# Up columns 3 to 20 of a diffusion layer: VectorE's work in one written-out order, the gated rows stored by ScalarE

## The chip, the core and the metric

The kernel runs on one NeuronCore of one Trainium2 chip, as one launch. The metric is the device time of that launch in microseconds (us). Five engines run side by side, each through its own queue in order: TensorE (PE in the profile; its weight loads are PEld), VectorE (DVE), ScalarE (ACT), GpSimd (POOL) and SyncE (SP, which here only issues DMAs). They meet at semaphores.

## What is computed

One layer of a bidirectional hybrid backbone, for 1024 tokens of a noisy latent grid (16 rows of 64) and 128 context tokens (the "prompt"), in float32 with 1024 features. Cut to the part that matters here, the channel mixer:

```
def dw_conv(u, conv_w, conv_b, grid):   # 3x3 over the 16x64 grid, or width 3 over the prompt
    ...
def conv_ffn(h, w_up, conv_w, conv_b, w_down, grid):
    u = dw_conv(h @ w_up, conv_w, conv_b, grid)     # w_up: 1024 x 5632
    gate, up = jnp.split(u, 2, axis=-1)             # 2816 hidden channels each
    return (jax.nn.silu(gate) * up) @ w_down        # w_down: 2816 x 1024
```

Before it come the two scan mixers with their projections, after it the gated residual and a last norm. All of that is the same before and after the change.

## The kernel before

**Stages.** The mixers and projections come first. The up stage (`h @ w_up`, the convolution, the gate) runs from about 768 us of the profiled span to 1260, the down stage (`@ w_down`) from there to the end.

**The up stage** goes over 22 hidden columns of 128 channels (`NHID`; the loop variable is `c`). Channels lie on the 128 partitions, tokens along the free axis. A column has a gate half and an up half, each a product of 1024 features by 128 channels by 1024 tokens. They are computed together, as a 2x2 block product with seven block products in place of eight (Strassen's scheme in Winograd's form), and each block product as three float32r products (high by high, high by low, low by high): 4 feature tiles x 3 = 12 matmuls of 512 tokens. In the trace these are line L1781, and their right-hand sides are named t1, t2, t3, t4, b11, b21, b22. The prompt's products are 24 matmuls of 256 columns a column of channels (L2030), turned by two transposes (L2047).

In the order of TensorE, which is one chain written out (`chained`), a stage of the loop holds: t1 (starts column c's gate half), the two transposes of column c-1's prompt, t4 (ends column c-1's up half), b21, b22, b11 (starts column c's up half), 12 prompt matmuls, t2, 12 prompt matmuls, t3. The last stage, c = 21, puts b11 between the two halves of b22.

**PSUM.** Each half of a column takes one of three buffers `u` in turn. So t1 of column c takes the buffer of column c-2's up half, and b11 of column c that of column c-1's gate half. TensorE's first weight load of t1 therefore waits for VectorE's last tap on column c-2's up half, and that of b11 for its last tap on column c-1's gate half.

**Per column on the other engines.** ScalarE copies three partial sums out of PSUM (`copy`, L1992: p1 after b11, u2 after t2, p5 after t1), makes each half's middle tap with the bias (`conv_middle`, L1946, 1024 tokens; for the prompt in `conv_prompt`, L1977), splits weights into high parts (L1763), and applies Silu to the gate (L2072). VectorE adds the copies back (p1: L2166, u2: L2167, p5: L2196), makes the eight other taps of each half as multiply-adds into an SBUF tile `acc` (`conv_rest`, L1964; taps 0 to 7 run over the kernel's rows and columns without the middle, so taps 3 and 4 have 1008 elements, 1 and 6 have 960, the corners 945), and two prompt taps for each half (L1981, 127 elements). Only after the u2 addition can the gate half's taps begin; the up half's need the p5 addition and t4. GpSimd makes the low parts of the weights (L69) and their sums (L1772 to L1775), multiplies Silu(gate) by up (`second_gate`, L2074), issues the store of the gated rows to DRAM (`scr_g`, L2075), moves one of the down weights' sums (L1911 to L1927) and forms sums over token halves of two columns (L1907 to L1911).

**What sets the order.** The program is recorded in Python's order and a scheduler orders each engine's queue from it; `tc.issue_after(x)` fixes that what follows is issued behind x. TensorE's order is written out; VectorE's, ScalarE's and GpSimd's in columns 3 to 20 are the scheduler's. The convolution's calls for a stage are these:

```
taps = prompt_columns(c - 1)
up(c - 1, 4)
second_half(c - 1)          # second_conv: conv_rows(up half); then second_gate
...
nc.vector.tensor_tensor(S[:, 512:NS], S[:, 0:512], copies["p5"], op=ALU.add)
...
anchor["conv"] = conv_rows(F, c, acc[c][0])
```

`F` is the gate half in PSUM, `S` the up half. `acc` tiles are four, reused two or three columns later.

## Time and profile before

| | us |
|---|---|
| median of 3 runs (lowest, highest) | 1509.09 (1507.84, 1511.35) |
| the profiled execution's own time | 1513.81 |
| its span, first to last instruction | 1512.0 |
| busy in the span: TensorE, VectorE, ScalarE, GpSimd | 1468.2, 1139.9, 782.4, 709.9 |
| 851 to 1234 (383 us, 17 stages of the up loop): TensorE, VectorE, ScalarE, GpSimd busy | 383.0, 371.7, 178.5, 372.7 |
| the same stretch: granted TensorE clock, DMA engines' busy share | 1.00, 0.54 |
| 1234 to 1271 (37 us, the change to the down stage): TensorE, VectorE busy | 34.1, 36.4 |

How to read the rows that follow: a timeline row has start, duration, engine, line, operation, what it writes <- what it reads, shape, and `x` the number of equal instructions that it merges; in brackets the idle time before it and what ended it. A matmul's record runs past the start of the next, since matmuls are pipelined, so distances are taken from start to start. A waits row has the waiting engine and line, what it waited for, the total, the count and the longest.

### The profile page before, as it was taken

What the parts mean: (1) busy time and instruction counts of PE and PEld (TensorE: products, weight loads), DVE (VectorE), ACT (ScalarE), POOL (GpSimd) and SP (SyncE); (2) the same over time, 40 slices, a digit from 0 to 9 for tenths busy, and PEclk for the clock granted to TensorE, in tenths of its full rate; (3) what the DMA queues carried; (4) which work ended last, traced back from release to release, by engine and by line L of the source; (5) the groups of instructions that cost most, each with busy time, mean ns of one, the idle gap of its engine ahead of it and who ended that gap; (6) DMA issues with size and microseconds to landing.
All of it is one profiled execution on the core that took longest, in us unless ns stands there. A gap on an engine that the chain in (4) does not pass through costs nothing.

```text
span 1512.0 us, 31135 instructions
## 1 busy us (share of the span) xinstructions
PE 1468.2 (97%) x12509; PEld 1251.9 (83%) x12509; DVE 1139.9 (75%) x1728; ACT 782.4 (52%) x1524; POOL 709.9 (47%) x541
## 2 busy tenths in 40 slices
PE   6999999999999999999999999999999999999998
PEld 2799998999898988777788888888888877888886
DVE  3766565674565767755799999999999999689475
ACT  3665567555454555513775444444444444466444
POOL 1612122334333241222339999999999996000001
PEclk9999999999999999999999999999999999999999
DMA  9311121335535363967652655554654667979762
GB/s 338 137 44 48 39 61 54 113 102 186 147 105 176 116 195 129 335 230 253 205 175 91 193 148 146 139 138 121 197 124 130 173 175 203 381 254 370 236 192 115
DMA packets 173802, 253.79 MB, mean 168 GB/s; under 512 B 11828, under 2 KB 113698, under 8 KB 171738
## 3 DMA queue, kind: packets, MB, share of 16 engines
q1 hardware_dynamic: 150455, 173.52, 36.0%
q0 software_dynamic: 22592, 77.60, 16.7%
q8 instruction: 98, 1.61, 0.4%
q10 hardware_dynamic: 611, 0.68, 0.1%
q14 instruction: 46, 0.38, 0.1%
HBM read 191.93 MB, written 82.90 MB: 182 GB/s over the span
## 4 chain that ended last, share of the span: by engine, by line
PE 81%; DMA 5%; DVE 4%; ACT 3%; POOL 3%; issue 2%; SPq 0%; POOLq 0%; ACTq 0%; DVEq 0%
PE u L1781 24%; PE mm L625 15%; PE xb L2317 7%; PE mm L639 6%; PE yb L2317 6%; PE x L2030 4%; PE mm L777 3%; PE lv L964 3%; PE yb L2371 2%; PE u L1545 2%; PE x L1032 2%; PE mm L519 1%; DMA raw<-in_w_in_dram 1%; PE ada L1201 1%; DMA wa<-in_w_ada_dram 1%
## 5 line engine op out<-in xcount | busy, mean ns | idle before, releaser
L1964 DVE SCALAR_TENSOR_TENSOR acc<-u,convc,acc 128x945 f32<-128x945 f32 (+2 forms) x352 | 426.6, 1218 | 7.4 <-ACT acc L1946 0.5
L69 POOL TENSOR_TENSOR wl<-raw,wh 128x1024 fp32r<-128x1024 f32 x42 | 102.9, 2462 | 248.3 <-ACT wh L133 193.1
L625 PE MATMUL mm<-h1h,wh 128*128 128x384 f32 x528 | 185.1, 350 | 0.9 <-ACT qj L528 0.9
L625 PE MATMUL mm<-h1l,wh 128*128 128x384 f32 x528 | 179.0, 339 | 0.0
L625 PE MATMUL mm<-h1h,wl 128*128 128x384 f32 x528 | 179.0, 339 | 0.0
L927 DVE TENSOR_TENSOR Q<-Q,fb 128x384 f32<-128x384 f32 x126 | 83.9, 666 | 84.6 <-PE lv L964 83.9
L69 POOL TENSOR_TENSOR wul<-ra,wuh 128x1024 fp32r<-128x1024 f32 (+1 forms) x45 | 113.2, 2516 | 22.2 <-ACT wuh L1763 15.7
L69 POOL TENSOR_TENSOR wul<-sr,wuh 128x512 fp32r<-128x512 f32 (+1 forms) x64 | 115.9, 1812 | 6.6 <-ACT wuh L1763 6.5
L917 ACT ACTIVATE m<-k 128x384 f32<-128x384 f32 x126 | 70.2, 557 | 82.4 <-PE lv L964 38.6
L2281 POOL TENSOR_TENSOR sq<-sq,mhalf 128x1 f32<-128x1 f32 x9 | 11.0, 1230 | 207.4 <-DVE sq L2280 207.4
L625 PEld LDWEIGHTS mm<-h1h,wh 128*128 128x128 f32 x528 | 99.4, 188 | 5.7 <-issue 3.9
L625 PEld LDWEIGHTS mm<-h1l,wh 128*128 128x128 f32 x528 | 99.5, 189 | 0.6 <-issue 0.2
L625 PEld LDWEIGHTS mm<-h1h,wl 128*128 128x128 f32 x528 | 99.3, 188 | 0.8 <-issue 0.5
L639 PE MATMUL mm<-wh,h1h 128*128 128x256 f32 x288 | 84.4, 293 | 0.0
L929 DVE TENSOR_TENSOR k<-k,fb 128x384 f32<-128x384 f32 x126 | 74.1, 588 | 10.8 <-ACT m L917 6.0
L639 PE MATMUL mm<-wh,h1l 128*128 128x256 f32 x288 | 81.2, 282 | 0.0
L639 PE MATMUL mm<-wl,h1h 128*128 128x256 f32 x288 | 81.0, 281 | 0.0
L133 ACT ACTIVATE wh<-raw 128x1024 fp32r<-128x1024 f32 x50 | 52.8, 1058 | 37.4 <-PE mm L625 11.8
L1992 ACT ACTIVATE u2p<-u 128x512 f32<-128x512 f32 x44 | 26.4, 599 | 71.1 <-PE u L1781 70.1
L2074 POOL TENSOR_TENSOR acc<-acc,acc 128x1152 f32<-128x1152 f32 x22 | 60.3, 2742 | 6.1 <-DVE acc L1964 4.9
L1763 ACT ACTIVATE wuh<-ra 128x1024 fp32r<-128x1024 f32 (+1 forms) x43 | 44.4, 1034 | 34.7 <-issue 15.7
L1763 ACT ACTIVATE wuh<-sr 128x512 fp32r<-128x512 f32 (+1 forms) x63 | 48.7, 773 | 22.6 <-PE x L2030 17.1
(385 smaller groups left out, 4471.6 us busy)
## 6 DMA issues: line engine op xcount, KB each, us to landing
ra<-in_w_ffn_up_dram SPq DMA_DIRECT2D x84, 256.0 KB, 3.1
raw<-in_w_in_dram SPq DMA_DIRECT2D x32, 512.0 KB, 4.6
v<-in_w_ada_dram SPq DMA_DIRECT2D x27, 512.0 KB, 4.9
scr_g<-acc POOLq DMA_DIRECT2D x22, 576.0 KB, 6.2
scr_s<-late POOLq DMA_DIRECT2D x11, 1024.0 KB, 8.1
scr_t<-in_w_ffn_down_dram POOLq DMA_DIRECT2D x16, 704.0 KB, 7.4
wa<-in_w_ada_dram SPq DMA_DIRECT2D x16, 512.0 KB, 5.9
scr_t<-in_w_ffn_down_dram POOLq DMA_DIRECT2D x2, 2816.0 KB, 12.6
```

What stands on the lines that cost most here:

```text
L69: return eng.tensor_tensor(out, full, hi.bitcast(F32), op=ALU.subtract)
L625: anchor["fill"] = mm(ps, a[:, kt, :], h[kt][b], start=(n == 0), stop=(n == 23))
L639: anchor["fill"] = mm(ps, h[kt][t // 3][:, ts_], a[:, kt % 4, :], start=(n == 0), stop=(n == 23))
L917: nc.scalar.activation(aps(t, 0, [[2 * h, NB], [h, 2], [1, h]]), aps(src, 0, [[2 * h, NB], [BL + h, 2], [1, h]]), AF.Copy)
L927: nc.vector.tensor_tensor(qm, qm, aps(ff_, 2 * h - 1, [[BL - h, 2], [2 * h, NB], [0, h]]), op=ALU.mult)
L929: nc.vector.tensor_tensor(km, km, aps(ff_, BL + 2 * h - 1, [[-(BL + h), 2], [2 * h, NB], [0, h]]), op=ALU.mult)
L1763: return lambda: nc.scalar.activation(hi, raw, AF.Copy), lambda eng: split_lo(eng, lo, raw, hi)
L1781: last = mm(dst, w_slot(c, a, x)[:, kt, :], HB[y][b][:, kt, :], start=(start and n == 0), stop=(stop and n == 11), skip_group_check=True,)
L1964: last = nc.vector.scalar_tensor_tensor(o, u3[:, r0 + dy : r1 + dy, c0 + dx : c1 + dx], wc(3 * (dy + 1) + dx + 1), o, op0=ALU.mult, op1=AL ...
L2030: last = mm(pk, HB[h]["p"][:, 4 * half + kt, :], aps(flat(W[x]), a * 512 + kt * P, [[(b - a) * 512, 2], [1, P]]), start=(half + kt + n == ...
L2074: last = anchor["gate"] = nc.gpsimd.tensor_tensor(accg, accg, accu, op=ALU.mult)
L2317: anchor["down"] = mm(banks[i][:, cs], w[a][:, ts_], w[b][:, 512 + cs.start : 512 + cs.stop], start=(start and j == 0 and n == 0), stop=(j ...
```

## The change

It concerns columns 3 to 20 (`FIXED`). Their VectorE instructions are issued in one chain (`vec`): each one is recorded behind the one before. `conv_prompt` is cut into its middle and its two taps, so that they can be placed apart. The gate half's prompt taps stay on either side of the gate's tap 3; the up half's two prompt taps move from the gate's last taps to behind the up half's taps 0 and 1; and the up half's tap 3 moves ahead of the p1 addition. ScalarE makes the gate half's middle tap ahead of the split of the weights s2 and s4 (before, behind it). The store of column c-1's gated rows goes from GpSimd's queue, where it stands some instructions behind the product, to ScalarE's queue, where it stands ahead of column c's Silu; columns 20, 21 and 0 to 2 keep the store on GpSimd. No instruction of TensorE or SyncE moves, and no operation is added or taken away.

VectorE's queue, from the gate half's tap 4 of column 15 (tile acc_10300) to the next column's p1 addition (`u<-u,cp`); acc_10299 is column 15's up half. Before:

```order
L1964 SCALAR_TENSOR_TENSOR acc_10300<-u,convc,acc_10300 128x16x63
L1964 SCALAR_TENSOR_TENSOR acc_10300<-u,convc,acc_10300 128x15x63
L1981 SCALAR_TENSOR_TENSOR acc_10299<-x,convc,acc_10299 128x127
L1964 SCALAR_TENSOR_TENSOR acc_10300<-u,convc,acc_10300 128x960
L1981 SCALAR_TENSOR_TENSOR acc_10299<-x,convc,acc_10299 128x127
L1964 SCALAR_TENSOR_TENSOR acc_10300<-u,convc,acc_10300 128x15x63
L1964 SCALAR_TENSOR_TENSOR acc_10299<-u,convc,acc_10299 128x15x63
L1964 SCALAR_TENSOR_TENSOR acc_10299<-u,convc,acc_10299 128x960
L1964 SCALAR_TENSOR_TENSOR acc_10299<-u,convc,acc_10299 128x15x63
L2166 TENSOR_TENSOR u<-u,cp_10253 128x512
```

The same piece of the changed kernel:

```order
L1964 SCALAR_TENSOR_TENSOR acc_10300<-u,convc,acc_10300 128x16x63
L1964 SCALAR_TENSOR_TENSOR acc_10300<-u,convc,acc_10300 128x15x63
L1964 SCALAR_TENSOR_TENSOR acc_10300<-u,convc,acc_10300 128x960
L1964 SCALAR_TENSOR_TENSOR acc_10300<-u,convc,acc_10300 128x15x63
L1964 SCALAR_TENSOR_TENSOR acc_10299<-u,convc,acc_10299 128x15x63
L1984 SCALAR_TENSOR_TENSOR acc_10299<-x,convc,acc_10299 128x127
L1964 SCALAR_TENSOR_TENSOR acc_10299<-u,convc,acc_10299 128x960
L1984 SCALAR_TENSOR_TENSOR acc_10299<-x,convc,acc_10299 128x127
L1964 SCALAR_TENSOR_TENSOR acc_10299<-u,convc,acc_10299 128x15x63
L1964 SCALAR_TENSOR_TENSOR acc_10299<-u,convc,acc_10299 128x16x63
L2075 TENSOR_TENSOR u<-u,cp_10253 128x512
```

The gate's last tap comes two instructions sooner, and one tap more (the up half's tap 3) stands before the p1 addition. From the p1 addition to the gate's tap 4 the order is the old one, without that tap. The changed order is the same in each of the 17 stages.

ScalarE's queue in the changed kernel, from the gate half's middle tap of column 15 to the next p1 copy:

```order
L1946 ACTIVATE acc_10300<-u,vcol,convc 128x1024
L1763 ACTIVATE wuh<-sr 128x2x512
L1763 ACTIVATE wuh<-sr 128x512
L2000 ACTIVATE u2p_10305<-u 128x512
L1976 ACTIVATE acc_10300<-x,vcol,convc 128x128
L1763 ACTIVATE wuh<-ra 128x2x512
L1946 ACTIVATE acc_10299<-u,vcol,convc 128x1024
L1976 ACTIVATE acc_10299<-x,vcol,convc 128x128
L2091 DMA scr_g_133<-acc_9783 128x1152
L2092 ACTIVATE acc_10300<-acc_10300 128x1152
L2000 ACTIVATE cp_10253<-u 128x512
```

Before, the first two rows stand the other way round and the DMA row is missing; acc_9783 holds column 14's gated rows.

The diff:

```diff
--- before.py
+++ after.py
@@ -1971,16 +1971,24 @@
             )
         return last
 
+    def prompt_middle(pp, ch, acc):
+        bc = vcol[:, col["conv_b"] + ch : col["conv_b"] + ch + 1]
+        return nc.scalar.activation(
+            acc[:, NS:NT], pp, AF.Identity, bias=bc, scale=convc[:, 4 * 44 + ch : 4 * 44 + ch + 1]
+        )
+
+    def prompt_tap(pp, ch, acc, dx):
+        c0, c1 = max(0, -dx), min(P, P - dx)
+        o = acc[:, NS + c0 : NS + c1]
+        t = (4 + dx) * 44 + ch
+        return nc.vector.scalar_tensor_tensor(
+            o, pp[:, c0 + dx : c1 + dx], convc[:, t : t + 1], o, op0=ALU.mult, op1=ALU.add
+        )
+
     def conv_prompt(pp, ch, acc):
-        wc = lambda t: convc[:, t * 44 + ch : t * 44 + ch + 1]
-        bc = vcol[:, col["conv_b"] + ch : col["conv_b"] + ch + 1]
-        nc.scalar.activation(acc[:, NS:NT], pp, AF.Identity, bias=bc, scale=wc(4))
+        prompt_middle(pp, ch, acc)
         for dx in (-1, 1):
-            c0, c1 = max(0, -dx), min(P, P - dx)
-            o = acc[:, NS + c0 : NS + c1]
-            nc.vector.scalar_tensor_tensor(
-                o, pp[:, c0 + dx : c1 + dx], wc(3 + dx + 1), o, op0=ALU.mult, op1=ALU.add
-            )
+            prompt_tap(pp, ch, acc, dx)
 
     u, pks = {}, {}
 
@@ -2039,6 +2047,58 @@
 
         chained(products)
 
+    FIXED = range(3, NHID - 1)
+
+    def vec(fn):
+        with tc.issue_after(anchor["vec"].ins) if "vec" in anchor else nullcontext():
+            anchor["vec"] = fn()
+
+    def gate_tap(c, i):
+        vec(lambda: conv_rest(u[c][0], c, acc[c][0], part=slice(i, i + 1)))
+
+    def up_tap(c, i):
+        vec(lambda: conv_rest(u[c][1], 22 + c, acc[c][1], part=slice(i, i + 1)))
+
+    def turn_prompt(c):
+        pp = ps_p.tile([P, 2, P], F32, name="x", tag="x")
+
+        def turned():
+            for i in range(2):
+                last = nc.tensor.transpose(pp[:, i, :], pt_t[:, i * P : (i + 1) * P], ident)
+            return last
+
+        chained(turned)
+        up_first = SLOT[c]["21"] < SLOT[c]["11"]
+        return (pp[:, 1 if up_first else 0, :], c, acc[c][0]), (pp[:, 0 if up_first else 1, :], 22 + c, acc[c][1])
+
+    def add_to(dst, a, nm):
+        return nc.vector.tensor_tensor(dst, a, copies[nm], op=ALU.add)
+
+    def fixed_rest(c):
+
+        gate_p, up_p = turn_prompt(c)
+        up(c, 4)
+        prompt_middle(*gate_p)
+        prompt_tapped(gate_p, -1)
+        gate_tap(c, 3)
+        prompt_tapped(gate_p, 1)
+        for i in range(4, 8):
+            gate_tap(c, i)
+        conv_middle(u[c][1], 22 + c, acc[c][1])
+        last = prompt_middle(*up_p)
+        if c - 1 in FIXED:
+            with tc.issue_after(last.ins):
+                nc.scalar.dma_start(scr_g[c - 1], gs[c - 1])
+        nc.scalar.activation(acc[c][0], acc[c][0], AF.Silu)
+        for i, dx in enumerate((-1, 1)):
+            up_tap(c, i)
+            prompt_tapped(up_p, dx)
+        up_tap(c, 2)
+        up_tap(c, 3)
+
+    def prompt_tapped(pp, dx):
+        vec(lambda: prompt_tap(*pp, dx))
+
     def prompt_columns(c):
         pp = ps_p.tile([P, 2, P], F32, name="x", tag="x")
 
@@ -2068,11 +2128,13 @@
     def second_gate(c):
 
         accg, accu = acc[c]
-        with after("p1") if c == 0 else nullcontext():
-            nc.scalar.activation(accg, accg, AF.Silu)
+        if c not in FIXED:
+            with after("p1") if c == 0 else nullcontext():
+                nc.scalar.activation(accg, accg, AF.Silu)
         gs[c] = accg
         last = anchor["gate"] = nc.gpsimd.tensor_tensor(accg, accg, accu, op=ALU.mult)
-        nc.gpsimd.dma_start(scr_g[c], accg)
+        if c + 1 not in FIXED or c not in FIXED:
+            nc.gpsimd.dma_start(scr_g[c], accg)
         if sums_todo and c > 0:
             with tc.issue_after(last.ins):
                 sums_todo.pop(0)()
@@ -2116,6 +2178,8 @@
             up(c - 1, 4)
             prompt_columns(c - 1)
             second_half(c - 1)
+        elif c - 1 in FIXED:
+            fixed_rest(c - 1)
         elif c > 0:
             taps = prompt_columns(c - 1)
             up(c - 1, 4)
@@ -2161,6 +2225,14 @@
             up(c, 7)
             up_prompt(c, 0)
             first_sums()
+        elif c - 1 in FIXED:
+            vec(lambda: add_to(F[:, 0:512], F[:, 0:512], "p1"))
+            up_tap(c - 1, 4)
+            up_tap(c - 1, 5)
+            vec(lambda: add_to(F[:, 512:NS], F[:, 512:NS], "u2"))
+            up_tap(c - 1, 6)
+            up_tap(c - 1, 7)
+            second_gate(c - 1)
         else:
             with after("second") if c < 3 else nullcontext():
                 nc.vector.tensor_tensor(F[:, 0:512], F[:, 0:512], copies["p1"], op=ALU.add)
@@ -2183,8 +2255,10 @@
             run("act", copy_pt)
         else:
             copy_pt()
+        if c in FIXED:
+            anchor["mid"] = conv_middle(F, c, acc[c][0])
         if c > 0 and n:
-            with tc.issue_after(anchor["copy"].ins) if c == 1 else nullcontext():
+            with after("mid") if c in FIXED else tc.issue_after(anchor["copy"].ins) if c == 1 else nullcontext():
                 split_slots(n, ("s2", "s4"), nc.gpsimd)
         if c == 1:
             with tc.issue_after(anchor["copy"].ins):
@@ -2193,8 +2267,14 @@
         if c > 0:
             if not last_c:
                 up(c, 7)
-            nc.vector.tensor_tensor(S[:, 512:NS], S[:, 0:512], copies["p5"], op=ALU.add)
-        if c > 0:
+            if c in FIXED:
+                gate_tap(c, 0)
+                vec(lambda: add_to(S[:, 512:NS], S[:, 0:512], "p5"))
+                gate_tap(c, 1)
+                gate_tap(c, 2)
+            else:
+                nc.vector.tensor_tensor(S[:, 512:NS], S[:, 0:512], copies["p5"], op=ALU.add)
+        if c > 0 and c not in FIXED:
             with after("second") if c < 3 else nullcontext():
                 anchor["conv"] = conv_rows(F, c, acc[c][0])
         if c > 0 and n:
```

## The prediction

> **What bounds the kernel now.** I read the page, then the table by stages, the list of waits in the up stage, and last the timelines of one stage on each engine. First the page's head, the row by stages for 851 to 1234 (time, then busy us and count of TensorE, weight loads, VectorE, ScalarE, GpSimd, granted clock, DMA share, GB/s), and two rows of the waits between 828 and 1300:
>
> ```profile
> span 1512.0 us, 31135 instructions
> 851.00:1234.00 383.00, 383.00 (x1875) 317.02 (x1874) 371.70 (x393) 178.48 (x240) 372.68 (x249) 1.00 0.54 149
> PEld u L1781 <- DVE acc L1964: 7.9, 18, 1.7
> PEld u L1781 <- PE u L1781: 4.6, 18, 0.3
> ```
>
> By busy time TensorE has nothing to give: 383.0 of 383. But its records overlap, and a weight load that waits shows only as a gap between loads. There are 18 such waits on a VectorE tap, one a stage, and 18 more that the profile puts down to TensorE itself. So I go by distances from start to start (TensorE; the last row is stage 21):
>
> ```profile
> 817.18 0.39 PE L1781 MATMUL u<-b11h,wuh 128*128 128x512 f32 x1
> 819.90 0.28 PE L2030 MATMUL x<-wuh,ph 128*128 128x256 f32 x1
> ...
> 851.33 0.47 PE L1781 MATMUL u<-t1h,wuh 128*128 128x512 f32 x1
> ...
> 1110.08 0.50 PE L1781 MATMUL u<-b11h,wuh 128*128 128x512 f32 x1
> 1112.95 0.28 PE L2030 MATMUL x<-wuh,ph 128*128 128x256 f32 x1
> 1121.29 0.47 PE L1781 MATMUL u<-t1h,wuh 128*128 128x512 f32 x1
> 1124.10 0.27 PE L2047 MATMUL x<-ident,late 128*128 128x128 f32 x1
> 1132.52 0.50 PE L1781 MATMUL u<-b11h,wuh 128*128 128x512 f32 x1
> 1233.68 0.47 PE L1781 MATMUL u<-t1h,wuh 128*128 128x512 f32 x1
> 1245.01 0.50 PE L1781 MATMUL u<-b11h,wuh 128*128 128x512 f32 x1 [1.28 <-DVE acc L1964]
> ```
>
> From the t1 of stage 4 to that of stage 21 there are 17 stages in 1233.68 - 851.33 = 382.35 us, 22.49 each. In stage 2, where b11 found its buffer free, its twelve matmuls took 819.90 - 817.18 = 2.72. In the stage shown the same twelve took 2.87 (1110.08 to 1112.95), and t1's twelve 2.81 (1121.29 to 1124.10). From b11 to b11 that stage took 22.44. Without those two stalls (0.15 and 0.09) it would take 22.20; the matmul ahead of each is stretched by some hundredths too, so 22.16 to 22.20 is TensorE's own pace (an estimate from these rows).
>
> Who is late is seen on VectorE, over the same stretch:
>
> ```profile
> 1113.78 0.70 DVE L2166 TENSOR_TENSOR u<-u,cp 128x512 f32<-128x512 f32 x1 [0.15 <-ACT cp L1992]
> ...
> 1118.10 0.69 DVE L2167 TENSOR_TENSOR u<-u,u2p 128x512 f32<-128x512 f32 x1
> 1118.70 3.69 DVE L1964 SCALAR_TENSOR_TENSOR acc<-u,convc,acc 128x960 f32<-128x960 f32 x3
> 1122.30 0.69 DVE L2196 TENSOR_TENSOR u<-u,u2p 128x512 f32<-128x512 f32 x1
> 1122.90 2.45 DVE L1964 SCALAR_TENSOR_TENSOR acc<-u,convc,acc 128x960 f32<-128x960 f32 x2
> 1125.28 0.35 DVE L1981 SCALAR_TENSOR_TENSOR acc<-x,convc,acc 128x127 f32<-128x127 f32 x1
> ...
> 1126.98 2.49 DVE L1964 SCALAR_TENSOR_TENSOR acc<-u,convc,acc 128x1008 f32<-128x1008 f32 x2
> 1129.62 0.35 DVE L1981 SCALAR_TENSOR_TENSOR acc<-x,convc,acc 128x127 f32<-128x127 f32 x1 [0.15 <-ACT acc L1977]
> 1129.89 1.21 DVE L1964 SCALAR_TENSOR_TENSOR acc<-u,convc,acc 128x960 f32<-128x960 f32 x1
> 1131.02 0.34 DVE L1981 SCALAR_TENSOR_TENSOR acc<-x,convc,acc 128x127 f32<-128x127 f32 x1
> 1131.27 4.79 DVE L1964 SCALAR_TENSOR_TENSOR acc<-u,convc,acc 128x945 f32<-128x945 f32 x4
> 1136.21 0.70 DVE L2166 TENSOR_TENSOR u<-u,cp 128x512 f32<-128x512 f32 x1
> ```
>
> The gate's last tap is the first of the four at 1131.27; at 1.19 it ends at 1132.46, and b11 begins at 1132.52. That closes a loop: p1 addition at 1113.78, gate's last tap done 18.68 later, b11 0.06 after that, its 2.87, the copy by ScalarE, next p1 addition at 1136.21. Round it takes 22.43, and **this loop, not a full engine, sets the stage**. VectorE itself waits twice in it, at 1129.62 and before 1136.21 (the four taps end at 1136.06). A tap that is followed by an unrelated instruction hands over 0.08 before its record ends (1129.89 + 1.21 against 1131.02), so each 0.15 of idle is 0.23 lost, and VectorE's own work is about 22.43 - 0.46 = 21.97. It fits under TensorE's 22.2.
>
> **The change part by part.** I call a the time at which the p1 addition could start if only TensorE and ScalarE decided; in the stage shown it is 1113.78. ScalarE's rows there:
>
> ```profile
> 1117.31 0.60 ACT L1992 ACTIVATE u2p<-u 128x512 f32<-128x512 f32 x1 [1.17 <-PE u L1781]
> ...
> 1119.00 1.06 ACT L1763 ACTIVATE wuh<-sr 128x1024 fp32r<-128x1024 f32 x1
> 1119.95 1.20 ACT L1946 ACTIVATE acc<-u,vcol,convc 128x1024 f32<-128x1024 f32 x1
> ...
> 1124.79 0.45 ACT L1977 ACTIVATE acc<-x,vcol,convc 128x128 f32<-128x128 f32 x1
> ...
> 1129.15 0.45 ACT L1977 ACTIVATE acc<-x,vcol,convc 128x128 f32<-128x128 f32 x1
> 1132.56 1.17 ACT L2072 ACTIVATE acc<-acc 128x1152 f32<-128x1152 f32 x1 [2.97 <-DVE acc L1964]
> ```
>
> 1. *VectorE's order up to b11.* Two times are fixed by TensorE through ScalarE: the u2 addition not before 1117.31 + 0.60 + 0.03 = 1117.94, a + 4.16; the gate's first prompt tap not before 1124.79 + 0.45 + 0.04 = 1125.28, a + 11.50, or a + 11.41 once t1 has lost its 0.09. From the u2 addition the order is the old one: 4.20 to the p5 addition (1118.10 to 1122.30), 2.98 to the first prompt tap (to 1125.28); that is a + 11.34, so it waits until 11.41. Then 1.70 to behind the second prompt tap (1125.28 to 1126.98) and now four gate taps in a row: 2.49 for two, and 2.45 - 1.21 = 1.24 for each of two more, 4.97. The gate is done at a + 18.09 instead of 18.68. The two prompt taps and their wait are gone from in front of it: 0.6 sooner. With a stage of 22.20, b11's load is due at a + 22.20 - 0.83 (b11's end to a, 1112.95 to 1113.78) - 2.72 - 0.23 (a load runs one matmul ahead, 2.72/12) = a + 18.42. The tap's end plus the 0.06 gives 18.15. **Spare 0.27: the wait of b11 goes.**
>
> 2. *VectorE's order round to the next p1 addition.* From the gate's last end: -0.08, tap 1.12 (3.60 for the three of 1118.70, less two at 1.24), prompt 0.26, tap 1.13 (1129.89 to 1131.02), prompt 0.26, two taps 2.41 (2.49 less 0.08): 5.10. So the p1 addition comes at a + 23.19, 0.99 behind the next a. Then 0.61 and two taps, 2.41: the u2 addition could start 4.01 after that a, and is held until 4.16. VectorE keeps up, with 0.15 to spare.
>
> 3. *t1.* Its buffer is freed by the up half's tap 7, the second of the three at 1118.70, which ends at 1121.15, a + 7.37. Now that is a + 4.16 + 0.60 + 1.24 + 1.20 = 7.20. 0.17 sooner against a stall of 0.09: it goes too, though with little to spare.
>
> 4. *ScalarE's middle tap sooner.* It moves ahead of a weight split of 1.06: it can start at 1119.00 instead of 1119.95 and is done at 1120.20, a + 6.42, and the split ends 1.1 later. The gate's tap 0, which needs the middle, comes at a + 4.16 + 0.60 + 2 x 1.24 = 7.24: no wait. GpSimd gets the high parts 1.1 later; see 5.
>
> 5. *The store.* GpSimd's rows, and a store issued by ScalarE elsewhere in the program:
>
> ```profile
> 1124.37 2.71 POOL L2074 TENSOR_TENSOR acc<-acc,acc 128x1152 f32<-128x1152 f32 x1
> 1132.59 1.04 POOL L2075 DMA_DIRECT2D scr_g<-acc  x1
> 40.07 0.36 ACTq L578 DMA_DIRECT2D scr_lr<-lrs  x1
> ```
>
> On ScalarE one issue costs between 0.36 and GpSimd's 1.04; I take 0.4, the row of the same engine. It stands between 1129.60 and the Silu at 1132.56, which waits 2.97 for VectorE (2.4 in the new order): hidden. It waits for the product, done at 1127.08, 2.5 before it; behind it on ScalarE are the Silu and the p1 copy, a further 3.5 away (the copy is due 0.63 before the next a, at 1135.35; less 1129.6, 1.17 and 1.04). Without this cover of 6.0 every us of lateness would move a. GpSimd loses 1.04 of issue and its split work starts at most 1.1 later: as much as nothing. I take 0 for 4 and 5, with +0.2 a stage as the bad end if GpSimd falls behind, and no gain as the good end, since TensorE waits for neither.
>
> 6. *Stage 21.* Here b11 comes half a product sooner and waits 1.28 us (row 1245.01). The gate of column 20 is done 0.6 sooner: 0.6 gained.
>
> Sum: 17 x (22.49 - 22.20) = 4.9, plus 0.6: **5.5 us**. It has to pass the change to the down stage, where the chain of waits runs
>
> ```profile
> 1245.01 4.39 PE u L1781 x18
> ...
> 1251.87 2.85 DMA raw<-in_w_ffn_down_dram
> ```
>
> that is, from TensorE's own up products to the first down weights, so what starts it is what comes sooner. The profiled execution took 1513.8 (span 1512.0 and 1.8 around it), 4.7 above the median of the runs; less 5.5 it would be 1508.3, and the median 1509.1 becomes **1503.6 us**.
>
> **Rivals.**
> - *The wait only moves.* VectorE has 0.15 of spare at the u2 addition. If an instruction in 1. or 2. costs some tenths more (a wait for two semaphores, a prompt tap late), t1's load waits for tap 7 instead: a stage of 22.35 gives 17 x 0.14 + 0.6 = 3.0, 1506.1. For it: the 0.15. Against: the new order has the same number of taps that directly follow one of their own tile, eight a stage. Up to no gain, 1509.1.
> - *GpSimd becomes the pace (slower).* It is busy 372.7 of 383, 21.9 a stage. If the split that comes 1.1 later idles it each stage and the missing issue doesn't pay that back, its round grows to 22.7; after some columns the product is more than 6.0 late, the store holds ScalarE's p1 copy, and all follow: 17 x 0.2 = +3.4, 1512.5. The point is a round over 22.49. Against: 21.9 - 1.0 + 1.1 is 22.0.
> - *The gain is lost at the down stage*, if the down weights or their sums (moved by GpSimd's queue) come at their own pace: 1508.5. Against: the chain above has TensorE before the DMA.
> - *TensorE's pace is not 22.2.* If 2.72 for twelve matmuls were itself some stall that eases, VectorE's 21.97 would be the limit: 17 x 0.52 + 0.6 = 9.4, 1499.7. Against: the twelve of row 817.18 waited for nothing and took 2.72. The Trainium skill's page "TensorE: Matmul & The Clock Gate", section "Wait — 56ns, not 53.3ns?", puts a warm matmul of 512 columns at 215.7 ns; here it is 2.72/12 = 227 ns at a granted clock of 1.00, so the trace disagrees and decides; by the page's figure a stage would be shorter than VectorE's 21.97, which is this rival's time.
>
> **How the numbers follow.** Forecast 0.73; the wait only moves 0.14; GpSimd 0.05; lost at the down stage 0.05; TensorE faster 0.03. Range 1501.6 to 1508.2: below, TensorE at 22.16 (6.2 gained) and 1.3 for the scatter of a median of three (the runs shown lie 3.5 apart); above, the first rival to most of its way. About 0.2%, 3.0 us, is what a measurement tells from no change. Faster: the forecast but 0.02, the last rival, 0.03 of the first: 0.77. Slower: GpSimd and 0.01 of the first: 0.06. Same: 0.17.
>
> **What would show it.** Right: stages of 22.2 from t1 to t1; no wait of b11's load on VectorE from stage 4 to 20, b11's twelve matmuls at 2.72; VectorE's p1 addition about 1 us behind its copy, and a short wait for ScalarE at the u2 addition and the prompt tap; stage 21's wait near 0.7; ScalarE's wait before Silu shorter, with a DMA issue in it. Wrong: stages at 22.4 or more with t1's load waiting (first rival), GpSimd without idle time and ScalarE waiting for its product (second), or stages of 22.2 with the first down product no sooner (third).

## The result, and the profile after

| | before | after |
|---|---|---|
| median of 19 runs each, on one chip (lowest, highest), us | 1511.76 (1507.84, 1514.93) | 1505.80 (1501.69, 1508.60) |
| ratio after to before, 95% interval | | 0.9962 (0.9954 to 0.9970) |
| the profiled execution: span, us | 1512.0 | 1504.1 |
| t1 of stage 4 to t1 of stage 21, us | 382.35 | 378.40 |

The change is worth 0.38% (0.30 to 0.46), 5.7 us of 1510; 5.5 were forecast. The forecast median of 1503.6 is missed by 2.2: it was counted down from the median of the three runs that were shown, 1509.09, which lies 2.7 below that of the nineteen. What was forecast well is the difference between the kernels. The row by stages of the changed kernel for 849 to 1227 (columns as before):

```profile
849.00:1227.00 378.00, 377.11 (x1870) 318.45 (x1869) 369.15 (x392) 177.85 (x239) 361.61 (x232) 1.00 0.55 150
```

And its waits of TensorE's weight loads between 828 and 1300:

```profile
PEld u L1781 <- DVE u L2276: 2.5, 1, 2.5
PEld u L1781 <- DVE acc L1964: 2.2, 2, 1.1
PEld u L1781 <- POOL wul L69: 1.3, 1, 1.3
PEld u L1781 <- PE u L1781: 0.3, 1, 0.3
```

The 18 waits on a VectorE tap (7.9 us) have become two, in stages 3 and 21, outside the stretch of stages 4 to 20; the 18 that the profile put down to TensorE itself (4.6 us) have become one. Two are new, once each, 2.5 and 1.3 us: they come below. TensorE from start to start (rows picked out, as in the prediction):

```profile
849.21 0.47 PE L1781 MATMUL u<-t1h,wuh 128*128 128x512 f32 x1
...
1105.65 0.39 PE L1781 MATMUL u<-b11h,wuh 128*128 128x512 f32 x1
1108.38 0.28 PE L2038 MATMUL x<-wuh,ph 128*128 128x256 f32 x1
1116.69 0.40 PE L1781 MATMUL u<-t1h,wuh 128*128 128x512 f32 x1
1119.44 0.38 PE L2067 MATMUL x<-ident,late 128*128 128x128 f32 x2
1127.85 0.39 PE L1781 MATMUL u<-b11h,wuh 128*128 128x512 f32 x1
1227.61 0.40 PE L1781 MATMUL u<-t1h,wuh 128*128 128x512 f32 x1
```

b11 to b11 takes 22.20 in the stage shown, b11's twelve 2.73 (2.87 before), t1's twelve 2.75 (2.81 before). Seventeen stages take 378.40, 22.26 each; without stage 7, which took 23.36, the mean is 22.19. The reason is on GpSimd and TensorE:

```profile
914.76 1.31 POOL L1909 TENSOR_TENSOR late<-acc 128x512 f32<-128x512 f32 x1 [3.54 <-DMA scr_s<-late]
917.35 0.50 PE L1781 MATMUL u<-t1h,wul 128*128 128x512 f32 x1 [0.89 <-POOL wul L69]
```

GpSimd stood 3.54 us because a store of the token sums had not yet left their tile, and the low half of t1's weights, next in its queue, came late. A second execution of the same kernel (below) has no such stage, so it does not belong to the order: 1.2 us by chance in one execution.

VectorE over the stage shown, from its p1 addition to the next, and ScalarE beside it:

```profile
1110.20 0.69 DVE L2075 TENSOR_TENSOR u<-u,cp 128x512 f32<-128x512 f32 x1
1110.80 2.50 DVE L1964 SCALAR_TENSOR_TENSOR acc<-u,convc,acc 128x1008 f32<-128x1008 f32 x2
1113.37 0.70 DVE L2075 TENSOR_TENSOR u<-u,u2p 128x512 f32<-128x512 f32 x1
...
1118.04 2.44 DVE L1964 SCALAR_TENSOR_TENSOR acc<-u,convc,acc 128x960 f32<-128x960 f32 x2
1120.62 0.35 DVE L1984 SCALAR_TENSOR_TENSOR acc<-x,convc,acc 128x127 f32<-128x127 f32 x1
...
1122.32 6.09 DVE L1964 SCALAR_TENSOR_TENSOR acc<-u,convc,acc 128x1008 f32<-128x1008 f32 x5
1128.33 0.34 DVE L1984 SCALAR_TENSOR_TENSOR acc<-x,convc,acc 128x127 f32<-128x127 f32 x1
...
1132.38 0.69 DVE L2075 TENSOR_TENSOR u<-u,cp 128x512 f32<-128x512 f32 x1
```

```profile
1108.57 0.60 ACT L2000 ACTIVATE cp<-u 128x512 f32<-128x512 f32 x1 [2.19 <-PE u L1781]
...
1112.73 0.60 ACT L2000 ACTIVATE u2p<-u 128x512 f32<-128x512 f32 x1 [1.16 <-PE u L1781]
...
1120.13 0.45 ACT L1976 ACTIVATE acc<-x,vcol,convc 128x128 f32<-128x128 f32 x1
...
1122.62 0.33 ACTq L2091 DMA_DIRECT2D scr_g<-acc  x1
...
1127.39 1.17 ACT L2092 ACTIVATE acc<-acc 128x1152 f32<-128x1152 f32 x1 [2.46 <-DVE acc L1964]
```

The p1 copy ends at 1109.17, so a is 1109.21, and the p1 addition now comes 0.99 us behind a. Against the times worked out from a: u2 addition a + 4.16 (forecast 4.16), gate's first prompt tap a + 11.41 (11.41), next p1 addition a + 23.17 (23.19). The gate's last tap is the fourth of the five at 1122.32; the fifth, of 1.19, ends at 1128.41 and starts 0.08 before the fourth's record ends, so the gate is done at 1127.30, a + 18.09 (18.09). b11's load starts 0.31 us later without having waited. VectorE's own two waits can be read here too: the two taps before the u2 addition end at 1113.30, and it starts at 1113.37, 0.04 behind the end of ScalarE's copy; the two gate taps at 1118.04 end at 1120.48, and the prompt tap starts at 1120.62, 0.04 behind the end of ScalarE's middle tap. They are 0.07 and 0.14.

**The end of the up columns changed too, which nothing in the prediction speaks of.** GpSimd (POOL), VectorE and TensorE about column 21's end, first after, then before:

```profile
1238.28 0.50 PE L1781 MATMUL u<-b11h,wuh 128*128 128x512 f32 x1 [0.72 <-DVE acc L1964]
...
1247.99 2.39 POOL L69 TENSOR_TENSOR wul<-ra,wuh 128x1024 fp32r<-128x1024 f32 x1 [5.91 <-ACT wuh L133]
1248.03 3.43 DVE L69 TENSOR_TENSOR wl<-ra,wh 128x1024 fp32r<-128x1024 f32 x1
1253.23 0.50 PE L1781 MATMUL u<-t4h,wuh 128*128 128x512 f32 x1 [2.29 <-DVE u L2276]
```

```profile
1254.50 1.21 DVE L69 TENSOR_TENSOR wl<-ra,wh 128x1024 fp32r<-128x1024 f32 x1
1254.71 3.28 POOL L69 TENSOR_TENSOR wul<-ra,wuh 128x1024 fp32r<-128x1024 f32 x1 [6.51 <-DMA raw<-in_w_ffn_down_dram]
1268.40 2.77 POOL L69 TENSOR_TENSOR wul<-sr,wuh 128x1024 fp32r<-128x1024 f32 x1
1271.23 0.50 PE L2317 MATMUL xb<-wul,wuh 128*128 128x512 f32 x1 [1.77 <-POOL wul L69]
```

Here VectorE and GpSimd both make low halves of down weights, each a subtraction of two SBUF tiles. Before, VectorE's started 0.21 us ahead of GpSimd's: VectorE's took 1.21, GpSimd's 3.28 instead of 2.4. After, GpSimd's started 0.04 us ahead: it took 2.39 and VectorE's 3.43. Whoever is second takes longer by nearly as much as the first still has to run. The Trainium skill's page "SBUF — State Buffer", section "Who interferes with whom", says that a VectorE instruction with two SBUF inputs contends with a GpSimd instruction that reads SBUF, because its second input comes through a shared read interface, and that the order of issue decides who is blocked. These rows agree. VectorE's delay holds back column 21's p5 addition, and with it TensorE's t4 by 2.29 us. In exchange TensorE no longer waits for GpSimd's low half of the fourth down pair, where it had lost 1.77 us by its own row, 2.16 from matmul to matmul: having come 2.3 us later, it finds it ready. One stall took the other's place.

The two spans differ by 8.0, more than the change is worth. Stage 0 starts at 768.05 before and at 765.97 after: 2.1 us of work that nothing here touches. Some 1.6 lie in the down stage, where the execution before had a lower granted clock for a moment (the figure before the last two; its row for 1256 to 1300):

```profile
1256.00:1300.00 44.00, 42.19 (x185) 34.31 (x184) 38.80 (x32) 18.23 (x22) 27.35 (x15) 0.96 0.84 250
```

The same row of after:

```profile
1256.00:1300.00 44.00, 43.96 (x196) 36.04 (x194) 38.10 (x31) 19.43 (x22) 20.72 (x13) 1.00 0.90 279
```

From the first down matmul on, the execution before took 251.55, where a kernel below with the same wait and a clock of 1.00 (store_only) took 249.96. The 4.3 that are left and the 1.2 of stage 7 make 5.5. From here on stages are compared with stages and runs with runs, not spans.

### The profile page after: what moved, and what is told of

Same layout as the page of the kernel before. It is cut to its first block, busy times and chain, and to the rows that moved or that the text cites. A ratio compares the mean times of both kernels' runs of the same rounds, so it can differ in the third digit from the quotient of the medians.

```text
span 1504.1 us, 31108 instructions
## 1 busy us (share of the span) xinstructions
PE 1460.4 (97%) x12509; PEld 1251.7 (83%) x12509; DVE 1139.8 (76%) x1728; ACT 783.2 (52%) x1524; POOL 699.7 (47%) x524
## 4 chain that ended last, share of the span: by engine, by line
PE 80%; DVE 5%; DMA 5%; ACT 3%; issue 3%; POOL 2%; SPq 0%; POOLq 0%; ACTq 0%; DVEq 0%
PE u L1781 23%; PE mm L625 15%; PE xb L2397 8%; PE yb L2397 6%; PE mm L639 5%; PE x L2038 3%; PE mm L777 3%; PE lv L964 3%; PE yb L2451 2%; PE u L1545 2%; DVE acc L1964 2%; PE x L1032 2%; PE mm L519 2%; DMA wa<-in_w_ada_dram 1%; PE ada L1201 1%
```

## Experiments

The theory: b11's wait on VectorE's last gate tap, and with it t1's wait on the up half's last tap, is all that the change removed; the store and the middle tap are neutral. "Stage" is the mean over the 17 stages from stage 4's t1 to stage 21's, from each kernel's profile; the medians of one block come from one chip and share the runs of the kernel before.

| kernel | median, us (runs) | kernel before beside it (runs) | ratio, 95% | t1 of stages 4 and 21 | stage |
|---|---|---|---|---|---|
| prompt_back | 1509.26 (11) | 1510.21 (28) | 0.9994 (0.9984 to 1.0003) | 849.04, 1230.03 | 22.41 |
| tap3_back | 1506.70 (11) | | 0.9980 (0.9971 to 0.9990) | 847.67, 1227.20 | 22.33 |
| store_back | 1507.68 (6) | | 0.9972 (0.9960 to 0.9983) | 851.36, 1228.58 | 22.19 |
| store_only | 1510.02 (11) | | 0.9994 (0.9985 to 1.0003) | 847.05, 1229.17 | 22.48 |
| late_middle | 1505.67 (11) | 1510.75 (23) | 0.9971 (0.9962 to 0.9980) | 851.21, 1228.46 | 22.19 |
| extra_one | 1504.88 (6) | | 0.9972 (0.9960 to 0.9983) | 847.85, 1225.10 | 22.19 |
| end_after | 1504.37 (6) | | 0.9966 (0.9954 to 0.9978) | 848.53, 1225.84 | 22.20 |
| end_before | 1508.77 (11) | | 0.9988 (0.9977 to 0.9999) | 848.50, 1230.73 | 22.48 |
| after_again | 1505.19 (6) | 1510.57 (16) | 0.9970 (0.9959 to 0.9982) | 851.70, 1228.97 | 22.19 |
| wide | 1504.22 (5) | | 0.9955 (0.9942 to 0.9967) | 849.53, 1227.39 | 22.23 |
| extra_three | 1508.80 (10) | | 0.9990 (0.9979 to 1.0001) | 848.18, 1228.29 | 22.36 |

### The up half's prompt taps back among the gate's taps

```diff
-        for i in range(4, 8):
+        for i in range(4, 6):
             gate_tap(c, i)
         ...
+        for i in (6, 7):
+            prompt_tapped(up_p, 2 * i - 13)
+            gate_tap(c, i)
         nc.scalar.activation(acc[c][0], acc[c][0], AF.Silu)
-        for i, dx in enumerate((-1, 1)):
-            up_tap(c, i)
-            prompt_tapped(up_p, dx)
-        up_tap(c, 2)
+        for i in range(3):
+            up_tap(c, i)
```

> The changed kernel with one part undone: the two prompt taps of the up column go back among the gate's last taps (between taps 5, 6 and 7, as before the change); the rest of the order, the store on ScalarE and the early middle tap stay. Theory (b11 waited for VectorE's last gate tap, and moving these two taps behind it is what freed it): they put the gate's end back by 2 x 0.26 = 0.52 us, with 0.1 to 0.2 more if the prompt tap waits for ScalarE's middle tap again; b11's load has 0.30 us to spare in the changed kernel, so it waits 0.2 to 0.45 us in every stage from 4 to 20. Stages go from 22.19 back to 22.4 to 22.6, b11's twelve from 2.72 to 2.85, and the time from 1505.8 to 1509.5 to 1512, that is most of the gain is lost. Rival one (the gain comes from moving the store from GpSimd to ScalarE): 1505 to 1507, stages stay at 22.2. Rival two (the gain comes from the up column's fourth tap ahead of the first addition): the same, 1505 to 1507.

The gain is gone: 0.9994, an interval that holds 1; the median, 1509.26, lies just under the expected 1509.5. The stages are at 22.41, and the waits of TensorE's loads between 828 and 1300 say which half of the loss this is:

```profile
PEld u L1781 <- DVE acc L1964: 8.4, 19, 1.7
PEld u L1781 <- PE u L1781: 0.3, 1, 0.3
```

b11's wait on the gate's last tap is back in every stage, t1's is not. So the two prompt taps' place is worth 22.41 - 22.19 = 0.22 us a stage, and both rivals fall: the store and the early tap 3 are still in this kernel and save only 22.49 - 22.41 = 0.08.

### The up half's tap 3 back behind the p1 addition

```diff
         up_tap(c, 2)
-        up_tap(c, 3)
 ...
             vec(lambda: add_to(F[:, 0:512], F[:, 0:512], "p1"))
+            up_tap(c - 1, 3)
             up_tap(c - 1, 4)
```

> The changed kernel with the other part of VectorE's order undone: the up column's tap 3 goes back behind the p1 addition, so that the addition comes one tap (1.18 us) sooner in VectorE's order. Theory: the addition then starts as soon as ScalarE's copy is there, about 0.05 to 0.1 us after it rather than 1.0, VectorE stands still for 0.1 to 0.2 us there, and the u2 addition comes 0.2 us later than the 1.18 us it would gain; the gate's end moves by +0.1 to +0.3 us against its copy. b11's 0.30 us of spare is used up or nearly: stages of 22.2 to 22.35 and 1505.5 to 1508.5. Rival (only the prompt taps' place counts, tap 3 is neutral): 1505 to 1506.5 and stages of 22.19. Rival (tap 3 ahead of the addition is the whole gain): stages of 22.45 and 1510.

Time and stage lie inside what was expected, but the mechanism is another one. The waits of VectorE (849 to 1227) and of TensorE's loads (828 to 1300):

```profile
DVE u L2075 <- ACT cp L2000: 4.3, 17, 0.3
PEld u L1781 <- PE u L1781: 4.6, 18, 0.3
```

VectorE's two additions in one stage:

```profile
1108.10 0.70 DVE L2075 TENSOR_TENSOR u<-u,cp 128x512 f32<-128x512 f32 x1 [0.25 <-ACT cp L2000]
1112.43 0.69 DVE L2075 TENSOR_TENSOR u<-u,u2p 128x512 f32<-128x512 f32 x1
```

b11 does not wait at all. The p1 addition now waits for its copy (0.25 us, in all 17 stages), and with three taps between, the u2 addition comes 4.33 after it, 0.17 behind the a + 4.16 of the changed kernel. The up half's last taps follow the u2 addition, and t1 waits for them again, with the same 18 waits and 4.6 us as in the kernel before. So tap 3 ahead of the addition is what frees t1. Of the 0.14 a stage (22.33 - 22.19), 0.11 lies there: from start to start, in the mean of the stages, t3's twelve take 2.77 where the changed kernel has 2.75, and t1's 2.83 where it has 2.75, both as in the kernel before. The other 0.03 lies in t4's twelve (2.85 where the kernel before and the changed one have 2.83), for which no wait is listed; its cause stays open. The two parts, 0.22 and 0.11, make 0.33 where both together saved 0.30.

### The store: back on GpSimd, and alone on ScalarE

```diff
-        if c - 1 in FIXED:
-            with tc.issue_after(last.ins):
-                nc.scalar.dma_start(scr_g[c - 1], gs[c - 1])
 ...
-        if c + 1 not in FIXED or c not in FIXED:
-            nc.gpsimd.dma_start(scr_g[c], accg)
+        nc.gpsimd.dma_start(scr_g[c], accg)
```

> The changed kernel with the gated rows' stores put back on GpSimd's queue for all columns; VectorE's order and the early middle tap stay. Theory (the store's place is neutral): stages of 22.19 and 1505 to 1507; ScalarE's start of the up column's middle tap moves by up to 0.3 us with no one waiting for it. Rival (the store on ScalarE carries a part of the gain, because GpSimd has 0.6 us more per stage for the weights' low halves): 1508 to 1510, with TensorE waits for GpSimd's low halves in several stages.

In the other kernel the order is that of before, and the store alone goes to ScalarE:

```diff
-            conv_prompt(pp[:, 0 if up_first else 1, :], 22 + c, acc[c][1])
+            last = conv_prompt(pp[:, 0 if up_first else 1, :], 22 + c, acc[c][1])
+            if c - 1 in FIXED and c in FIXED:
+                with tc.issue_after(last.ins):
+                    nc.scalar.dma_start(scr_g[c - 1], gs[c - 1])
 ...
-        nc.gpsimd.dma_start(scr_g[c], accg)
+        if c + 1 not in FIXED or c not in FIXED:
+            nc.gpsimd.dma_start(scr_g[c], accg)
```

> The kernel before with only the stores moved from GpSimd to ScalarE (behind the up column's prompt middle tap), VectorE's order left to the planner as before. Theory (neutral): 1510.5 to 1513 with stages of 22.45 to 22.55 and b11's load waiting in every stage as before. Rival (the store is the gain): 1506 to 1508 with stages below 22.35.

The stages are 22.19 and 22.48: those of the changed kernel and of the kernel before. With the store alone the waits of TensorE's loads are the old ones:

```profile
PEld u L1781 <- DVE acc L1964: 8.0, 19, 1.7
PEld u L1781 <- PE u L1781: 4.6, 18, 0.3
```

The store's place is neutral in the stages. The medians miss a little: store_back lies 0.7 us over the expected 1507, with an interval that holds the changed kernel's ratio, and store_only, 1510.02, 0.5 under the expected 1510.5, with an interval that holds 1.

### ScalarE's middle tap back behind the split

```diff
-        if c in FIXED:
-            anchor["mid"] = conv_middle(F, c, acc[c][0])
         if c > 0 and n:
-            with after("mid") if c in FIXED else ...:
+            with ...:
                 split_slots(n, ("s2", "s4"), nc.gpsimd)
         ...
+            if c in FIXED:
+                conv_middle(F, c, acc[c][0])
```

> The changed kernel with ScalarE's middle tap of the gate's image rows put back behind the high half of slots s2 and s4 (1.05 us). Theory: VectorE's order needs the middle tap sooner, since gate tap 0 now starts 0.65 us after the middle tap's end; put back, gate tap 0 waits 0.3 to 0.5 us in every stage, of which VectorE's own slack (0.07 at the u2 addition, 0.13 at the prompt tap) and b11's spare 0.30 take most: stages 22.2 to 22.4 and 1506 to 1509. Rival, the step as forecast (the middle tap's place is worth nothing): stages of 22.19 and 1505 to 1506.5.

The stages stay at 22.19, so the theory here was wrong and the rival, the step as forecast, held. VectorE's waits between 849 and 1227 show why it was close:

```profile
DVE acc L1964 <- ACT acc L1946: 3.7, 16, 0.3
```

Gate tap 0 does wait now, some 0.2 us in 16 stages, and that is covered by the time in which VectorE would otherwise have waited at the prompt tap and by b11's spare.

### One and three more instructions ahead of the gate's end

```diff
         for i in range(4, 8):
+            if i == 7:
+                o = gate_p[0][:, 0:127]
+                vec(lambda: nc.vector.scalar_tensor_tensor(
+                    o, o, convc[:, c : c + 1], acc[c][0][:, NS : NS + 127], op0=ALU.mult, op1=ALU.add))
             gate_tap(c, i)
```

In the second kernel the condition is `i > 4`.

> The changed kernel with one more prompt-sized VectorE instruction (128 x 127, 0.26 us) ahead of the gate's last tap in columns 3 to 20; it writes a tile that nobody reads any more, so the results are the same. Theory: VectorE's work in a stage is 21.98 of 22.19 us; with 0.26 more it is 22.24 and becomes the pace, while b11's spare of 0.30 is just not used up: stages of 22.24 to 22.33, 1506.8 to 1508.3, and the wait is t1's load on the up column's last tap, not b11's. Rival (VectorE has more room than its two waits show): stages of 22.19, 1505 to 1506.5. Rival (b11's spare is smaller than its 0.30 us): b11's load waits in every stage, 22.4 and 1509.

It costs nothing, against the theory: 22.19. VectorE from the gate's tap 4 to the first prompt tap behind its end:

```profile
1119.78 3.75 DVE L1964 SCALAR_TENSOR_TENSOR acc<-u,convc,acc 128x1008 f32<-128x1008 f32 x3
1123.44 0.35 DVE L2089 SCALAR_TENSOR_TENSOR x<-x,convc,acc 128x127 f32<-128x127 f32 x1
1123.69 2.30 DVE L1964 SCALAR_TENSOR_TENSOR acc<-u,convc,acc 128x945 f32<-128x945 f32 x2
1125.91 0.35 DVE L1984 SCALAR_TENSOR_TENSOR acc<-x,convc,acc 128x127 f32<-128x127 f32 x1
```

From 1119.78 to 1125.91 are 6.13 us; in the changed kernel the same stretch is 1122.32 to 1128.33, 6.01. An instruction that takes 0.25 from its start to the next one's (1123.44 to 1123.69) has lengthened the chain by 0.12. It stands between two taps that write one tile, where the second had to wait for the end of the first; an unrelated instruction goes into that gap. 0.12 is less than VectorE's two waits, 0.07 and 0.14, together, and than b11's 0.31. What the room is then, three of them should tell:

> The changed kernel with three prompt-sized VectorE instructions more, one ahead of each of the gate's taps 5, 6 and 7 (they write a tile nobody reads any more). One of them cost nothing: it stood between two taps that depend on each other and took away 0.12 us of the pause between them, so that it added 0.14 us net, which the 0.20 us of VectorE's two waits covered. Theory: three add 3 x 0.14 = 0.42 us, 0.22 more than there is, and 0.12 more than b11's spare of 0.30: VectorE is the pace, stages of 22.35 to 22.45, b11 or t1 waits in every stage, 3 to 4.5 us above the changed kernel, 1508 to 1510. Rival (there is more room than the waits show): stages of 22.19 to 22.3 and at most 2 us more.

```profile
1122.22 1.26 DVE L1964 SCALAR_TENSOR_TENSOR acc<-u,convc,acc 128x1008 f32<-128x1008 f32 x1
...
1128.62 0.34 DVE L1984 SCALAR_TENSOR_TENSOR acc<-x,convc,acc 128x127 f32<-128x127 f32 x1
```

```profile
PEld u L1781 <- PE u L1781: 4.6, 18, 0.3
```

The same stretch takes 6.40, 0.39 more than in the changed kernel; the stages take 22.36, 0.17 more, and the time is 1508.8. That is as the theory had it: some 0.2 us of the 0.39 is room, the rest is the stage's. The wait that comes back is t1's, with the 18 and 4.6 us of the kernel before. From start to start 0.11 of the 0.17 lies at t1, 0.03 at b11 (its twelve take 2.75 instead of 2.72) and 0.03 in t4's twelve, as in tap3_back.

### The end of the up columns, in both kernels

```diff
-        return load_w([a, b], [2 * 512], nc.gpsimd if p == 1 and j < 6 else nc.vector)
+        key = "pairs" if p == 1 and j < 6 else "last_add" if p == 1 and j == 6 else None
+        return load_w([a, b], [2 * 512], nc.gpsimd if p == 1 and j < 6 else nc.vector, key)
 ...
             nc.scalar.activation(hi, raw, AF.Copy)
-            split_lo(eng, lo, raw, hi)
+            with after(key):
+                last = split_lo(eng, lo, raw, hi)
+            if key == "pairs":
+                anchor[key] = last
 ...
-                nc.vector.tensor_tensor(S[:, 512:NS], S[:, 0:512], copies["p5"], op=ALU.add)
+                anchor["last_add"] = nc.vector.tensor_tensor(S[:, 512:NS], S[:, 0:512], copies["p5"], op=ALU.add)
```

> The changed kernel with the work at the end of the up columns reordered, the stages themselves untouched: VectorE's low half of the seventh down pair (a subtraction of two tiles of SBUF that took 3.43 us in column 21, beside a GpSimd subtraction that had started 0.04 us before it, where its like take 1.22) goes behind column 21's last addition, and GpSimd makes the low half of the fourth down pair before those of the fifth and sixth. Theory (every kernel so far loses about 2.1 us once at this end, either in column 21 or at the fourth pair of the first down product, and both have GpSimd behind them): neither wait is left, 1503 to 1504.5, that is 1.8 to 2.3 us under the changed kernel and a ratio to the kernel before of 0.994 to 0.9952. Rival (the wait only moves on, to the fifth or sixth pair or to the first gated rows of the down stage): 1505 to 1506.5.

> The kernel before with the same reordering of the end, VectorE's order in the stages as before the change. Theory: the first down product's wait of 2.16 us for GpSimd's low half goes, 1507.5 to 1509 (ratio 0.998 to 0.9995), with stages still at 22.45 to 22.55. Against the changed kernel with the same end this leaves the stages alone: 17 x 0.30 = 5.1 and 0.6 of column 21, 5 to 6 us between the two. Rival (the changed kernel's gain lay partly at the end): less than 4 us between the two.

Which of the two ends a kernel has is decided by a few hundredths of a microsecond, as the profiles of all kernels without this edit show: VectorE's low half took 1.21 or 1.22 in seven of them, in which its start lay within 0.01 us of GpSimd's or ahead of it, and 3.43 or 3.44 in the three (the changed kernel twice, extra_three) where GpSimd's was 0.04 ahead. late_middle is the closest case, its rows beside those of the changed kernel above:

```profile
1249.00 1.22 DVE L69 TENSOR_TENSOR wl<-ra,wh 128x1024 fp32r<-128x1024 f32 x1
1249.01 3.49 POOL L69 TENSOR_TENSOR wul<-ra,wuh 128x1024 fp32r<-128x1024 f32 x1 [7.18 <-DMA raw<-scr_g]
```

The lengths of the end, from each profile (t1 of stage 21 to the first matmul of the first down product, and from there to the end of the span):

| | to the first down product | from there |
|---|---|---|
| before | 26.79 | 251.55 |
| store_only | 26.80 | 249.96 |
| late_middle | 26.53 | 249.93 |
| the changed kernel, twice | 28.61, 28.61 | 247.85, 247.83 |
| end_after | 26.10 | 248.95 |
| end_before | 26.77 | 249.03 |

The changed kernel pays 2.1 more than late_middle in the first part and 2.1 less in the second: between these two the trade is worth nothing. Over the kernels built from the changed one, both parts together take 276.0 to 277.0 where VectorE was first and 276.4 to 277.7 where it was second, so that a worth of some tenths is not excluded. In end_after and end_before neither of the two stalls is left, but a third to a half of the gain is given back later, which is what the rival described. The loads' wait of end_after:

```profile
PEld xb L2401 <- DVE wul L69: 1.3, 2, 1.0
```

That is the low half of the eighth and ninth down pairs, which VectorE makes behind column 21's taps. What remains is 276.46 - 275.05 = 1.4 us against the changed kernel, instead of the 1.8 to 2.3 expected. The medians cannot settle so little: 0.9966 for end_after, 0.9970 and 0.9962 for the changed kernel. (end_after's median, 1504.37, lies in the expected range, its ratio does not.) Between end_before and end_after, which have the same end, lie 5.7 us by the profiles from stage 4's t1 to the end of the span (658.0 and 652.4), inside the 5 to 6 expected; by the medians it is 4.4, between that and the rival's less than 4. So most of the gain, at the least, does not hang on how the end goes.

### The changed kernel again, and a longer range

> The changed kernel once more, beside the two below and the kernel before. Theory: the stall at the end of the up columns is the same in every kernel with this end (2.1 us at the first down product's fourth pair, or 2.3 us in column 21 in its place), and the stage of 23.36 us seen once (GpSimd late behind a store of the token sums) was a chance event: stages of 22.19 all through, 1505 to 1507, ratio to the kernel before 0.996 to 0.997. Rival (the late stage belongs to this order): again one stage above 23 us.

The second execution has stages of 22.16 to 22.28 all through, and again the 2.3 us in column 21. The late stage 7 was chance; the stall in column 21 came both times.

```diff
-    FIXED = range(3, NHID - 1)
+    FIXED = range(2, NHID - 1)
 ...
```

The reordered end of end_after is in this kernel too (its lines stand above).

> The changed kernel with the reordered end of the run before last (VectorE's low half of the seventh down pair behind column 21's last addition, GpSimd's low half of the fourth ahead of the fifth and sixth), and the written-out order from column 2 on instead of 3. Theory: stage 3, 23.11 us in every run so far with b11 waiting 0.63 us, loses that wait and goes to 22.2 to 22.4; with the 1 to 1.3 us of the end it is 1.7 to 2.2 us under the changed kernel beside it: 1503 to 1505, ratio to before 0.9945 to 0.9958. Rival (stage 3's time has other causes, or column 2's order costs as much in stage 2): within 1.3 us of the changed kernel.

Stage 3 goes from 23.15 in the kernel beside it to 22.45, just over the expected 22.2 to 22.4, and the stages behind it are 22.23 instead of 22.19: t4's twelve are the stretched ones of tap3_back, 2.85 instead of 2.83. Why stays open. Its ratio is the lowest measured here, 0.9955 (0.9942 to 0.9967) beside the changed kernel's 0.9970 (0.9959 to 0.9982): by the medians 1 us faster than the changed kernel and 6.4 than the kernel before, but the two intervals overlap, so that the first is likely and not shown, and how much of it is the longer range's and how much the end's is not separated.

## Why the prediction was right

**Step 1, VectorE's order up to b11**, held to the hundredth: the gate's end at a + 18.09, and prompt_back shows that this is what frees b11. The spare was put at 0.27, with a hand-over of 0.06 already taken off; in the stage shown it is 0.31 - 0.06 = 0.25.

**Step 2, the round to the next p1 addition**, held: 23.17 where 23.19 was worked out, the addition 0.99 behind a (0.99), and a short wait at the u2 addition as well as at the prompt tap. "VectorE's own work is about 21.97" counted the pauses between taps of one tile as work, which is right for this order; extra_one showed that part of them can be filled.

**Step 3, t1**, held in the result. tap3_back shows that the 0.17 of this step is real and comes from tap 3's new place: without it, t1 waits as before. That costs 0.11 us a stage, the 0.09 that was read off t1's twelve and 0.02 in the last matmul of t3. "With little to spare" was right too: t1's first load still starts 0.29 behind the load ahead of it (0.44 before the change), where loads are otherwise 0.23 apart. Its matmuls no longer feel that: the twelve take 2.75, and so do t2's in every kernel here.

**Steps 4 and 5, middle tap and store**, were costed at nothing and are worth nothing in the stages (late_middle and store_back, 22.19 both; store_only 22.48 against 22.49). Step 5's issue was put at 0.4 and took 0.33, and Silu's wait shrank from 2.97 to 2.46 with 2.4 foreseen. One sign did not come true: in 15 of the 17 stages the issue is not in that wait. In the stage shown it comes at 1122.62, 0.31 behind the end of GpSimd's product and ahead of ScalarE's middle taps, so it needed no cover from Silu's wait.

**Step 6, stage 21**, is the one that was mis-sized. b11's wait fell from 1.28 to 0.72 us, 0.56 where 0.6 was forecast, but the step ended there. In the same column the changed order let GpSimd go first at a shared read interface, and 2.29 us were lost at t4, hidden in the total only because a wait of about the same size at the first down product (1.77 by its row, 2.16 from matmul to matmul) went in the same moment. That the two cancel is luck. That product's wait stands in the profile before, and it wasn't counted; the third rival (the gain is lost at the down stage) is near it, but its mechanism, weights that come at their own pace, did not occur.

**The sum.** 17 x (22.49 - 22.19) = 5.1 for the stages where 4.9 was forecast; from t1 of stage 21 to the end of the span 276.77 (store_only, which has the waits of the kernel before at a clock of 1.00) less 276.46, 0.3, that is the 0.56 of b11 less what the trade took back: 5.4. The forecast of 5.5 was right in size and in its main parts, the stages above all; at the end it left out two terms that nearly cancel, by luck. The first rival (22.35 a stage, t1's load waiting) is what tap3_back built, at 22.33; it did not occur in the changed kernel because the order in step 2 cost no tenth more than worked out. GpSimd as the pace did not occur: its busy time fell, 361.6 of 378 us. TensorE faster than 22.2 did not occur: in every kernel with VectorE out of the way the stage is 22.19 (22.23 in wide).

## What to carry to other kernels

When two engines hand buffers round in a loop, work out the times from one anchor, instruction by instruction; with durations from the same trace this held to some hundredths here and showed which of two waits each move removes. Test each part by undoing it: the two that looked like one saving were two, on two loads. And follow the new order to its edge, where the loop ends and other work begins: a coincidence there, decided by 0.04 us, cost 2.3 us, two fifths of the gain, and was made good by luck alone.

## What the runs showed of the hardware that was not expected

- Two subtractions of SBUF tiles, one on VectorE and one on GpSimd, do not run side by side: the second took 3.43 us instead of 1.22 (VectorE) or 3.2 to 3.5 instead of 2.39 (GpSimd), depending on which started first.
- An unrelated VectorE instruction of 0.25 us between two taps of one tile lengthens the chain by 0.12; three lengthen it by 0.39.
- ScalarE's queue can issue a DMA ahead of the instructions that stand before it: the store of the row at 1122.62 stands behind the up half's two middle taps in the order, but these ran at 1123.40 and 1124.48 by ScalarE's timeline. It never came before GpSimd's product was done, but 0.02 to 1.02 us behind its end; what else releases it is not shown.
